# A decoder step's 24-column projection moved from a split weight stream to 16 fp32 matmuls in four column groups

## The chip, the cores and the metric

One core of a Trainium2 chip runs the kernel. The metric is the device time of one execution in microseconds. Three timed runs of the kernel before gave 1956.45, 1956.59 and 1956.63 us; their median is 1956.59.

## The reference

The reference is one layer of a hybrid recurrent decoder for 288 tokens: 256 of a prompt and 8 sequences of 4. The input `x` (288 x 2048) is normalised, scaled and shifted by a condition (the products of `silu(c)` with `w_ada`), and projected by one wide matrix. The projection is then cut into the inputs of three branches:

```
mod = silu(c) @ P['w_ada'] + P['b_ada']
xn = rmsnorm(x, P['g_norm1']) * (1.0 + sc1) + sh1
proj = xn @ P['w_in']
(lru_x, g_q, g_k, g_v, g_lr, g_gate, m_x, m_o, m_if, mg) = jnp.split(proj, _split_points(), axis=-1)
...
logdec = jax.nn.log_sigmoid((g_lr @ P['gla_w_g2'] + P['gla_b_g']).astype(jnp.float32)) / GLA_TAU
...
gates = (m_if + P['ml_b_if']).astype(jnp.float32)
```

All pieces but two are wide (512 to 6144 columns). The two narrow ones are `g_lr`, 16 columns, the low-rank input of the GLA branch's decay, and `m_if`, 8 columns, the input and forget gates of the four mLSTM heads. The change is about these 24 columns. The branches (a linear recurrence "LRU", gated linear attention "GLA" and an mLSTM) are then merged under gates, projected by `w_out`, and followed by a feed-forward block. All of it is in fp32.

## The kernel before

**Layout.** Features lie on the 128 partitions and the 288 tokens along the free axis. `x` is 16 k-tiles of 128 features each.

**Wide projections.** `stream` runs a weight block of 512 columns (four tiles `mm` in PSUM, 128 columns each) over the k-tiles in groups of two. A group's weights are loaded as one 512 KB tile `raw` (L155, `fetch`), split into a high part `hi` by ScalarE (ACT, L164) and a remainder `lo` by VectorE (DVE, L171, `halve`), and each 128 x 128 tile gets three products on TensorE (PE): hi times the high part of the activation (`xh`, L188), hi times its remainder (`xl`, L189) and lo times `xh` (L190). A group of the wide stream thus has 2 k-tiles x 4 column tiles x 3 = 24 products. `raw`, `hi` and `lo` have three buffers each. When a block's last product is done, DVE adds it to what earlier stages left (L576, `added_to`) or another function takes it up.

**Conditions.** The weights of the condition come in units of 1 MB (`fetch_pair`, loads at L381, L368 and L370) that go into spare slots: `ag`, two `st` tiles, or free `s` slots. The letters of a pattern such as `"L L L L . V . L L . V ."` say what `run` does after each group of the stream: L loads the next unit, V visits, that is, runs the products of all units held (fp32 matmuls at L331, four 32-column groups `j` of the array in turn), `.` does nothing. A slot is free for the next unit only when its visit has run.

**Stages.** The normalised `x` becomes final in six stages. In stages 2 to 5 the columns of q, k, v and the LRU's input are computed over the k-tiles of the stage; between the stages DVE and ACT turn the next k-tiles into `xh` and `xl` (L471 to L498). Stage 5 is the last; after it all 16 k-tiles are there. Then comes the narrow projection (`wsm`, one column tile of 128, of which 104 are zeros, 8 k-tiles in a 512 KB load, two loads), and then the "gate stage", the two blocks of `g_gate`, with the pattern `"L L L L . V . ."` and the slots 6, 7, `st` and `ag`. Beside these run the convolution (POOL and DVE, L667 to L686) and the LRU's recurrence as a side generator that moves on one step with each group.

**Who sets the order.** SyncE (SP) issues the loads in program order; a load whose target is still read waits, and all later loads on SP wait behind it. Loads ahead are thus limited by the order of the program. PE, ACT, DVE and POOL are ordered by a scheduler from the program's priorities.

**The narrow projection and its readers.** The lines, before the change, of the pieces that it touches:

- L771 to L772: `sm` and the `stream` over `wsm`; ACT's copy of the result into `sm`
- L868 on, `gla`: POOL clears the 128-partition tile `wg2` and loads its first 32 partitions; the products at L879 take `wg2` (16 rows of it hold the low-rank weight) and `sm`
- L1153 on, `gate_rows`: POOL makes a 0/1 selector `sel` from columns of `ident`; the product at L1158 takes one head's gate out of `sm` and spreads it over 32 partitions each
- the host's packing of `wsm` (2048 x 128, gates at columns 0, 1, 32, 33, 64, 65, 96 and 97, low-rank columns at 2 to 17) and of `wg2`

Of the kernel before, what the change touches and what calls it, by code (L numbers as in the profile page):

```python
# [8 lines left out]
F32 = mybir.dt.float32  # L9
# [5 lines left out]
P = 128  # L15
D = 2048
KT = D // P
# [4 lines left out]
N = NP + NS  # L22
EPS = 1e-6
BIG = 3.4028235e38
SH1, SC1, GT1, SH2, SC2, GT2 = range(6)
# [28 lines left out]
def trunk(ctx, tc, io):  # L54
# [18 lines left out]
    def nm(s):  # L73
        uid[0] += 1
        return f"{s}_{uid[0]}"
# [7 lines left out]
    def misc():  # L83
        return px.tile([P, 512], F32, tag="px", name=nm("px"))
# [157 lines left out]
    def run(gen):  # L242
        for _ in gen:
            if pace["every"]:
                if pace["n"] >= 0:
                    step(pace["every"][pace["n"] % len(pace["every"])])
                pace["n"] += 1
            for g in list(side):
                with tc.high_priority(), ExitStack() as behind:
                    for e in ("last", "lo", "hi"):  # L250
                        behind.enter_context(tc.issue_after(pace[e].ins))
                    if next(g, side) is side:
                        side.remove(g)
# [152 lines left out]
    def visit(n=99):  # L406

        for _ in range(min(n, len(held))):
            name, raw, products, end = held.pop(0)
            products(raw)  # L410
            if end:
                end()
                done.add(name)

    def step(cs):
        for c in cs:
            if c == "L":
                load_one()
            elif c == "F":
                fetched.append(fetch(*ahead_of.pop(0)))  # L420
            elif c.isdigit():
                with tc.high_priority(), tc.issue_after(pace["last"].ins):
                    visit(int(c))
            elif c == "V":
                with tc.high_priority(), tc.issue_after(pace["last"].ins):
                    visit()

    def drain(n):
        while n not in done:
# [126 lines left out]
    qk, vv, lx = slot(8), slot(9), slot(2)  # L556
    early = [(B_Q, qk, 0), (B_Q + 1, qk, 4), (B_Q + 2, vv, 0), (B_Q + 3, vv, 4), (B_LRU, lx, 0), (B_LRU + 1, lx, 4)]
    kept = []

    def start_of(j, onv=(0,)):  # L560

# [61 lines left out]

    a, w = COFF["eye"]
    for i, turn, p in ((2, (5, 4, 0, 1, 2, 3), "F2LL F1FL 2FLL 1 2 ."), (3, (3, 2, 1, 0, 4, 5), "L L . L LV . L L . LLV . ."),
                       (4, (5, 4, 0, 1, 2, 3), "L L . L LV . L L . LLV . ."), (5, (3, 4, 5, 0, 1, 2), "L L L L . V . L L . V .")):
        k0, k1, _ = STAGES[i]
        if i == 5:
            slots.update(ids=(3, 4, None, 5, 6, 7), n=0)
        pace.update(hpins=pace["copies"][-1:])  # L630
        lead = begin(i, p)
        if i < 5:
            with tc.issue_after(pace["lo"].ins):
                for k in range(k1, STAGES[i + 1][1], 2):
                    normalize(k, 2)
        if i == 2:
            ahead_of.extend((win, early[j][0], 1) for j in turn[1:])
            step("FLL")
        else:
            assert not held and not fetched and not ahead_of  # L640
        if i == 4:
            for t, n, r in ((con, "con", slice(0, a)), (con, "con", slice(a + w, CW)), (par, "par", slice(112, PW))):
                G.tensor_copy(t[:, r.start:r.start + 1], mod[:, SC1, 8, 0:1])
                G.dma_start(t[:, r], io[n][:, r])
        take, kept = kept, []
        xh1, mods = pace["xh"], pace["mod"]
        for n, j in enumerate(turn):
            pace["pins"] = pace["adds"][-5:-4] + [mods] * (n > 0)
            if n == 1:
                pace["hpins"] = [xh1]  # L650
            evac = start_of(5, (0, 2)) if i == 2 and n == 0 else added_to(j)
            run(stream(win, early[j][0], act1, k1, evac, k0=k0, take=None if n else take,
                       keep=kept if n == 5 and i < 5 else None, first=() if n else lead))
# [114 lines left out]
    lru_ = beside(lru())  # L768


    sm = cp.tile([P, N], F32, tag="sm", name="sm")  # L771
    run(stream(io["wsm"], 0, act1, KT, lambda m, p: S.copy(sm, p), width=P, kg=8))  # L772
    sg = slot(2)

    def gate_silu(base):
# [92 lines left out]
    def gla():  # L868
        kk_, g_cs, ee = slot(3), slot(4), slot(5)
        wg2 = flat(kk_)[:, 4 * N:4 * N + 512]  # L870
        G.memset(wg2, 0.0)
        G.dma_start(wg2[0:32], io["wg2"])
        rm = resets(row("gc"), 0.0, 1.0, 64)
        bg = Pm("bg")
        yield
# [273 lines left out]
    def gates():  # L1149
        lf, gc, ar, mr, rt = (row(n) for n in ("lf", "gc", "ar", "mr", "rt"))  # L1150
        one, big_ = resets(row("rr"), 0.0, 1.0, NP), None

        def gate_rows(i):  # L1153

            p = misc()
            sel = t288()[:, 0:P]
            G.tensor_copy(sel.rearrange("p (h i) -> p h i", h=4), ident.rearrange("p (h i) -> p h i", h=4)[:, :, i:i + 1].to_broadcast([P, 4, 32]))
            T.matmul(p[:, :N], sel, sm, start=True, stop=True)  # L1158
            return p

        pf = gate_rows(1)
        softlog(lf, pf[:, :N], Pm("bf"), rt)
        pI = gate_rows(0)
        V.tensor_scalar(ar, pI[:, :N], Pm("bi"), None, ALU.add)
        yield
        S.activation(rt, rt, AF.Exp, scale=-1.0)
        S.activation(rt, rt, AF.Ln, bias=1.0)
        yield
        V.tensor_tensor(out=lf, in0=lf, in1=rt, op=ALU.subtract)
        V.tensor_tensor_scan(gc, one, lf, 0.0, ALU.mult, ALU.add)  # L1170
        yield
        V.tensor_tensor(out=ar, in0=ar, in1=gc, op=ALU.subtract)
        big_ = resets(row("lf"), -BIG, 0.0, NP)
        m0 = Pm("m0")
        V.tensor_copy(rt, ar)
        V.tensor_scalar(rt[:, 0:1], ar[:, 0:1], 0.0, None, ALU.max)
        V.tensor_tensor(out=rt[:, NP:N:TS], in0=ar[:, NP:N:TS], in1=m0, op=ALU.max)
        yield
        V.tensor_tensor_scan(mr, big_, rt, 0.0, ALU.add, ALU.max)
        gm = gc  # L1180
        V.tensor_tensor(out=gm, in0=gc, in1=mr, op=ALU.add)
        yield
        mo_ = sc([P, 9], "mout", 1)
        G.tensor_copy(mo_[:, 0:1], gm[:, NP - 1:NP])
        G.tensor_copy(mo_[:, 1:9], gm[:, NP + 3:N:TS])
        G.dma_start(io["o_m"], mo_)
        xr = gm
        S.activation(xr, gm, AF.Exp, scale=-1.0)
        V.tensor_scalar(rt[:, 0:NP], ar[:, 0:NP], mr[:, NP - 1:NP], None, ALU.subtract)

        def bt(a):
            return a.rearrange("p (b t) -> p b t", b=NB)

        mrs = bt(mr[:, NP:N])
        V.tensor_tensor(out=bt(rt[:, NP:N]), in0=bt(ar[:, NP:N]), in1=mrs[:, :, 3:4].to_broadcast([P, NB, TS]), op=ALU.subtract)
        wr = rt
        S.activation(wr, rt, AF.Exp)
        yield
        srow = sc([P, 3, NS], "srow", 1)
        V.tensor_tensor(out=bt(srow[:, 2, :]), in0=m0.unsqueeze(2).to_broadcast([P, NB, TS]), in1=mrs, op=ALU.subtract)  # L1200
        S.activation(srow[:, 2, :], srow[:, 2, :], AF.Exp)
        V.tensor_copy(srow[:, 0, :], ar[:, NP:N])
        V.tensor_copy(srow[:, 1, :], wr[:, NP:N])
        csr = sc([P, NB], "csr", 1)
        V.tensor_copy(csr, srow[:, 2, 3:NS:TS])
        V.tensor_tensor(out=srow[:, 0:2], in0=srow[:, 0:2], in1=eye.unsqueeze(1).to_broadcast([P, 2, NS]), op=ALU.mult)
        scol = sc([P, 2], "scol", 1)
        V.tensor_reduce(out=scol, in_=srow[:, 0:2], axis=AX.X, op=ALU.add)
# [574 lines left out]
```

## Time and profile before

| | |
|---|---|
| median of 3 runs | 1956.59 us (1956.45 to 1956.63) |
| the profiled execution's own time | 1956.76 us |
| its span in the trace | 1955.0 us |
| granted TensorE clock | 0.998 |
| PE busy | 1931.4 us, 99% of the span |
| DVE, ACT, POOL busy | 1039.7, 810.4, 235.5 us |
| loads of the small projection | 198.3 and 201.0 us after the span's start |
| copy into `sm` | 220.0 us |
| first reader of `sm` (L879) | 328.4 us |

Times in the views count from the start of the span. In a timeline row the first number is the start in us, the second the time from the start of the row's first instruction to the end of its last, then engine, line, operation, output <- inputs, shapes, and how many instructions the row holds; brackets give the idle time of the engine ahead of the row and what ended it. An fp32 matmul shows as two instructions. PEld is the weight load of a product, SPq the issuing of a DMA. `128*32` in a PE row says that 32 of the array's columns are used at a time, `128*128` that all are.

### The profile page before, as it was taken

To read this page: it belongs to the slowest core of one execution; us is meant where nothing else is said; L and a number is where in the kernel's file an instruction comes from. 1 tells how busy PE (TensorE), PEld (TensorE's weight loads), DVE (VectorE), ACT (ScalarE), POOL (GpSimd) and SP (SyncE) were. 2 spreads that over 40 slices of the span, in tenths; PEclk is the share of its full clock that TensorE was granted. 3 is DMA by queue.
4 is the path that set the end of the run, shared out by engine and by line. 5 is a ranking of instruction groups with operands and counts; after the bars stand their busy time and mean duration, and the time that the engine had idled before them with its cause. 6 is when DMAs were issued, how large, how long until landed. Compare 5 with 4: busy or idle time off the path is not lost.

```text
span 1955.0 us, 35982 instructions
## 1 busy us (share of the span) xinstructions
PE 1931.4 (99%) x15084; PEld 1832.6 (94%) x15084; DVE 1039.7 (53%) x1601; ACT 810.4 (41%) x1127; POOL 235.5 (12%) x335
## 2 busy tenths in 40 slices
PE   7999999999999999999999999999999999999997
PEld 6899889998999999899999899999999999999997
DVE  6665737535673456654444564445454445444565
ACT  4333474444554353443333453443433334343433
POOL 0001000011042112000013330000000000010101
PEclk9999999999999999999999999999999999999999
DMA  9898566557443369876788554444444544444443
GB/s 391 355 349 318 216 253 234 204 183 258 158 163 119 131 204 311 282 260 251 280 316 322 182 205 162 162 162 164 168 171 154 175 173 162 162 162 162 162 167 119
DMA packets 110161, 417.01 MB, mean 213 GB/s; under 512 B 11648, under 2 KB 11824, under 8 KB 106288
## 3 DMA queue, kind: packets, MB, share of 16 engines
q1 hardware_dynamic: 100944, 382.34, 54.5%
q0 software_dynamic: 8048, 28.99, 4.4%
q10 hardware_dynamic: 1008, 3.39, 0.5%
q8 instruction: 118, 1.93, 0.4%
q14 instruction: 43, 0.35, 0.1%
HBM read 397.86 MB, written 16.81 MB: 212 GB/s over the span
## 4 chain that ended last, share of the span: by engine, by line
PE 97%; DVE 1%; DMA 1%; ACT 0%; issue 0%; SPq 0%; DVEq 0%; ACTq 0%
PE mm L188 29%; PE mm L190 28%; PE mm L189 28%; PE pa L331 5%; DMA s<-wad 1%; PE px L1436 0%; PE pi L1428 0%; PE px L735 0%; PE px L978 0%; PE px L1360 0%; PE px L128 0%; PE px L817 0%; DMA raw<-win 0%; PE px L1046 0%; PE px L1370 0%; PE pi L447 0%
## 5 line engine op out<-in xcount | busy, mean ns | idle before, releaser
L171 DVE TENSOR_TENSOR lo<-raw,hi 128x1024 fp32r<-128x1024 f32 x450 | 550.4, 1225 | 547.2 <-ACT hi L164 517.6
L164 ACT ACTIVATE hi<-raw 128x1024 fp32r<-128x1024 f32 x446 | 472.1, 1060 | 801.7 <-PE mm L189 607.3
L188 PE MATMUL mm<-xh,hi 128*128 128x288 f32 x2544 | 749.4, 299 | 0.3 <-ACT xh L473 0.3
L189 PE MATMUL mm<-xl,hi 128*128 128x288 f32 x2544 | 745.7, 296 | 0.3 <-DVE xl L475 0.3
L190 PE MATMUL mm<-xh,lo 128*128 128x288 f32 x2544 | 730.6, 295 | 0.1
L188 PEld LDWEIGHTS mm<-xh,hi 128*128 128x128 f32 x2544 | 474.7, 188 | 19.1 <-issue 10.9
L188 PE MATMUL mm<-s,hi 128*128 128x288 f32 x1664 | 490.6, 297 | 0.0
L189 PE MATMUL mm<-s,hi 128*128 128x288 f32 x1664 | 488.2, 295 | 0.0
L189 PEld LDWEIGHTS mm<-xl,hi 128*128 128x128 f32 x2544 | 476.9, 188 | 2.4 <-DVE xl L475 0.6
L190 PE MATMUL mm<-s,lo 128*128 128x288 f32 x1664 | 476.6, 295 | 0.4 <-DVE lo L171 0.4
L190 PEld LDWEIGHTS mm<-xh,lo 128*128 128x128 f32 x2544 | 472.0, 188 | 1.8 <-issue 0.8
L188 PEld LDWEIGHTS mm<-s,hi 128*128 128x128 f32 x1664 | 311.8, 188 | 5.2 <-issue 4.6
L189 PEld LDWEIGHTS mm<-s,hi 128*128 128x128 f32 x1664 | 312.5, 188 | 0.3
L190 PEld LDWEIGHTS mm<-s,lo 128*128 128x128 f32 x1664 | 308.3, 188 | 0.8 <-DVE lo L171 0.7
L171 DVE TENSOR_TENSOR lo<-s,hi 128x1024 fp32r<-128x1024 f32 x80 | 98.0, 1225 | 113.8 <-ACT hi L164 113.8
L164 ACT ACTIVATE hi<-s 128x1024 fp32r<-128x1024 f32 x80 | 84.9, 1061 | 140.8 <-PE mm L189 140.1
L1612 POOL TENSOR_TENSOR t<-t 128x288 f32<-128x288 f32 x64 | 60.2, 951 | 639.2 <-ACT t L1611 639.2
L576 DVE TENSOR_TENSOR s<-s,mm 128x288 f32<-128x288 f32 x92 | 39.6, 450 | 48.0 <-PE mm L190 47.4
L1628 DVE TENSOR_TENSOR s<-s,mm 128x288 f32<-128x288 f32 x96 | 40.2, 449 | 33.8 <-PE mm L190 32.6
L1132 POOL TENSOR_TENSOR s<-s,t 128x288 f32<-128x288 f32 x32 | 33.9, 1090 | 191.6 <-DVE t L1131 191.5
L331 PE MATMUL pa<-s,silc 128*32 128x64 f32 (+3 forms) x832 | 52.9, 373 | 0.2 <-DMA s<-wad 0.2
L498 DVE TENSOR_TENSOR s<-t,s 128x288 fp32r<-128x288 f32 x64 | 33.8, 568 | 15.5 <-ACT s L497 15.5
(403 smaller groups left out, 1153.4 us busy)
## 6 DMA issues: line engine op xcount, KB each, us to landing
raw<-win SPq DMA_DIRECT2D x188, 512.0 KB, 4.8
raw<-wf SPq DMA_DIRECT2D x176, 512.0 KB, 4.2
s<-wf SPq DMA_DIRECT2D x80, 512.0 KB, 3.5
s<-wada SPq DMA_DIRECT2D x26, 1024.0 KB, 8.0
s<-wad SPq DMA_DIRECT2D x24, 1024.0 KB, 10.1
ag<-wada SPq DMA_DIRECT2D x22, 1024.0 KB, 5.5
raw<-wout SPq DMA_DIRECT2D x32, 512.0 KB, 5.3
st<-wada SPq DMA_DIRECT2D x20, 512.0 KB, 7.2
```

Source lines behind the costliest of these rows:

```text
L164: pace["hi"] = S.activation(hi, raw, AF.Copy)
L171: pace["lo"] = V.tensor_tensor(out=lo[:, r], in0=raw[:, r], in1=hi[:, r].bitcast(F32), op=ALU.subtract)
L188: T.matmul(pss[m][:, :N], hi[:, kk, ms], xh, start=k == k0 and not take, stop=False)
L189: T.matmul(pss[m][:, :N], hi[:, kk, ms], xl, start=False, stop=False)
L190: pace["last"] = T.matmul(pss[m][:, :N], lo[:, kk, ms], xh, start=False, stop=k == kt - 1 and keep is None)
L331: pace["prod"] = T.matmul(ps[32 * j:32 * j + 32, h * w // 4:(h + 1) * w // 4], silu_c(k), v[:, j], start=k == 0 and h == 0, stop=k == KT - ...
L498: pace["mod"] = V.tensor_tensor(out=dst_l[:, r], in0=src[:, r], in1=dst_h[:, r].bitcast(F32), op=ALU.subtract)
L576: pace["adds"].append(V.tensor_tensor(out=dst[:, base + m, :], in0=dst[:, base + m, :], in1=p, op=ALU.add))
L1132: G.tensor_tensor(out=a, in0=a, in1=t, op=ALU.add)
L1612: G.tensor_tensor(out=r, in0=r, in1=r, op=ALU.mult)
L1628: V.tensor_tensor(out=a, in0=a, in1=p, op=ALU.add)
```

## The change

The stream over `wsm` goes. In its place a function `narrow` runs 16 plain fp32 matmuls, one for each k-tile, of 32 columns by 288 tokens. K-tile `k` goes to the column group `k % 4`, so that PSUM's partitions 0 to 31 hold the sum over the k-tiles 0, 4, 8 and 12, the next 32 that over 1, 5, 9 and 13, and so on. The four partial sums are never added by an instruction of their own: the whole 128-partition tile is copied to `sm`, and the consumers' products add them, because their other operand is repeated four times (`wg2` by the host, the selector by `eye[:, i:8:2]` broadcast).

`narrow` is called by a new letter N in stage 5's pattern, right behind the first visit. Its input is the unsplit activation `xin(k)`. Its weights (16 x 32 columns, 256 KB) are loaded into an `st` tile by SP ahead of stage 5's first group. Line numbers behind the insertion move by 11 to 14 (L576 becomes L588, L772's copy L437).

```diff
+            elif c == "N":
+                with tc.high_priority(), tc.issue_after(pace["prod"].ins):
+                    narrow()
...
+    def narrow():
+
+        ps = misc()
+        for k in range(KT):
+            j = k % 4
+            T.matmul(ps[32 * j:32 * j + 32, :N], ws[:, k], xin(k), start=k < 4, stop=k >= KT - 4, skip_group_check=True)
+        S.copy(sm, ps[:, :N])
...
-                       (4, (5, 4, 0, 1, 2, 3), "L L . L LV . L L . LLV . ."), (5, (3, 4, 5, 0, 1, 2), "L L L L . V . L L . V .")):
+                       (4, (5, 4, 0, 1, 2, 3), "L L . L LV . L L . LLV . ."), (5, (3, 4, 5, 0, 1, 2), "L L L L . VN . L L . V .")):
         if i == 5:
             slots.update(ids=(3, 4, None, 5, 6, 7), n=0)
+            ws = sp.tile([P, 1028], F32, tag="st", name=nm("st"), bufs=2)[:, 0:512].rearrange("p (k c) -> p k c", k=KT)
+            Q.dma_start(ws, io["wsm"])
...
-    sm = cp.tile([P, N], F32, tag="sm", name="sm")
-    run(stream(io["wsm"], 0, act1, KT, lambda m, p: S.copy(sm, p), width=P, kg=8))
...
-        G.memset(wg2, 0.0)
-        G.dma_start(wg2[0:32], io["wg2"])
+        G.dma_start(wg2, io["wg2"])
...
-            G.tensor_copy(sel.rearrange("p (h i) -> p h i", h=4), ident.rearrange("p (h i) -> p h i", h=4)[:, :, i:i + 1].to_broadcast([P, 4, 32]))
+            G.tensor_copy(sel.rearrange("p (h i) -> p h i", h=4), eye[:, i:8:2].unsqueeze(2).to_broadcast([P, 4, 32]))
...
-    wsm = np.concatenate([wi[:, 6160:6161], wi[:, 6164:6165], wi[:, 3072:3088], z[:, :14], wi[:, 6161:6162], wi[:, 6165:6166], z,
-                          wi[:, 6162:6163], wi[:, 6166:6167], z, wi[:, 6163:6164], wi[:, 6167:6168], z], 1)
+    wsm = np.zeros((D, 32), np.float32)
+    wsm[:, 0:8] = wi[:, 6160:6168].reshape(D, 2, 4).transpose(0, 2, 1).reshape(D, 8)
+    wsm[:, 8:24] = wi[:, 3072:3088]
...
-        "wg2": np.pad(I["gla_w_g2"][0], ((2, 14), (0, 0))),
+        "wg2": np.tile(np.pad(I["gla_w_g2"][0], ((8, 8), (0, 0))), (4, 1)),
```

The change moves instructions at three places on which the prediction's steps rest. The first is SP's order at the end of stage 4 and the start of stage 5. `raw_…<-win` is a 512 KB group of a wide projection, `s…<-wada` a condition unit. Before:

```order
L155 DMA raw_1968<-win 128x1024
L155 DMA raw_1998<-win 128x1024
L155 DMA raw_2046<-win 128x1024
L370 DMA s_288_2077<-wada 128x2x1024
L155 DMA raw_2079<-win 128x1024
L370 DMA s_292_2113<-wada 128x2x1024
```

The same place now:

```order
L155 DMA raw_1969<-win 128x1024
L155 DMA raw_1999<-win 128x1024
L643 DMA st_2029<-wsm 128x512
L155 DMA raw_2049<-win 128x1024
L370 DMA s_289_2080<-wada 128x2x1024
L155 DMA raw_2082<-win 128x1024
```

The load of the narrow weights has come in ahead of stage 5's first group (`raw_2046`, now `raw_2049`), and its target is one of the `st` tiles that the visit at the end of stage 4 reads.

The second place is SP's order from the end of stage 5 into the gate stage. Before (`raw_2586` is the gate stage's first group, `s_366` the first condition unit loaded in it):

```order
L155 DMA raw_2454<-win 128x1024
L155 DMA raw_2490<-wsm 128x1024
L155 DMA raw_2546<-wsm 128x1024
L155 DMA raw_2586<-win 128x1024
L370 DMA s_366_2616<-wada 128x2x1024
L155 DMA raw_2626<-win 128x1024
L370 DMA s_370_2656<-wada 128x2x1024
L155 DMA raw_2662<-win 128x1024
```

The same place now (`raw_2514` is the gate stage's first group, `s_358` its first condition unit):

```order
L155 DMA raw_2475<-win 128x1024
L155 DMA raw_2514<-win 128x1024
L370 DMA s_358_2544<-wada 128x2x1024
L155 DMA raw_2572<-win 128x1024
L370 DMA s_365_2602<-wada 128x2x1024
L155 DMA raw_2608<-win 128x1024
```

The two `wsm` groups are gone, so one group stands ahead of the first condition unit behind stage 5's last group, where three stood.

The third place is DVE's order in stage 5, where one block ends and the next begins. The L576 rows add the four column tiles `mm` of the block that ends, and `lo_2193` is the remainder of the next block's first group. Before:

```order
L576 TENSOR_TENSOR s_47_276<-s_47_276,mm_2115 128x288
L576 TENSOR_TENSOR s_47_276<-s_47_276,mm_2116 128x288
L171 TENSOR_TENSOR lo_2193<-raw_2191,hi_2192 128x1024
L576 TENSOR_TENSOR s_47_276<-s_47_276,mm_2117 128x288
L171 TENSOR_TENSOR lo_2223<-raw_2221,hi_2222 128x1024
L576 TENSOR_TENSOR s_47_276<-s_47_276,mm_2118 128x288
```

The same place now, with L588 for the adds and `lo_2196` for that remainder:

```order
L588 TENSOR_TENSOR s_47_276<-s_47_276,mm_2118 128x288
L588 TENSOR_TENSOR s_47_276<-s_47_276,mm_2119 128x288
L588 TENSOR_TENSOR s_47_276<-s_47_276,mm_2120 128x288
L588 TENSOR_TENSOR s_47_276<-s_47_276,mm_2121 128x288
L171 TENSOR_TENSOR lo_2196<-raw_2194,hi_2195 128x1024
L171 TENSOR_TENSOR lo_2226<-raw_2224,hi_2225 128x1024
```

All four adds now stand ahead of the remainder.

More of the change, by code (lines that the diff above doesn't have):

```diff
@@ L558, in trunk @@
     kept = []
+    sm = cp.tile([P, N], F32, tag="sm", name="sm")
     def start_of(j, onv=(0,)):
@@ L1744 @@
         "lst": np.ascontiguousarray(flat(fm(I["state_lru_conv"][0]))), "mst": np.ascontiguousarray(flat(fm(I["state_mlstm_conv"][0]))),
-        "wg2": np.pad(I["gla_w_g2"][0], ((2, 14), (0, 0))),
+        "wg2": np.tile(np.pad(I["gla_w_g2"][0], ((8, 8), (0, 0))), (4, 1)),
         "x": np.ascontiguousarray(fm(x)), "ct": np.ascontiguousarray(fm(c)), "par": np.ascontiguousarray(par), "con": _consts(),
-        "wada": np.ascontiguousarray(I["w_ada"][0].reshape(KT, P, 6, 2, 1024).transpose(2, 3, 0, 1, 4)[GT1:]), "wad1": wad1, "win": pack(win), "wsm": pack(wsm, P),
+        "wada": np.ascontiguousarray(I["w_ada"][0].reshape(KT, P, 6, 2, 1024).transpose(2, 3, 0, 1, 4)[GT1:]), "wad1": wad1, "win": pack(win), "wsm": np.ascontiguousarray(wsm.reshape(KT, P, 32).transpose(1, 0, 2)),
         "lruw": np.ascontiguousarray(np.concatenate([I["lru_w_a"][0], I["lru_w_x"][0]], 0).transpose(1, 0, 2)).reshape(P, 2048),
```

## The prediction

> **What bounds the kernel now.** I read the page first: the engines' busy shares, the chain of waits by engine, and the cost rows of the operations that prepare weights.
>
> ```profile
> PE 1931.4 (99%) x15084; PEld 1832.6 (94%) x15084; DVE 1039.7 (53%) x1601; ACT 810.4 (41%) x1127; POOL 235.5 (12%) x335
> ...
> PE 97%; DVE 1%; DMA 1%; ACT 0%; issue 0%; SPq 0%; DVEq 0%; ACTq 0%
> ...
> L171 DVE TENSOR_TENSOR lo<-raw,hi 128x1024 fp32r<-128x1024 f32 x450 | 550.4, 1225 | 547.2 <-ACT hi L164 517.6
> L164 ACT ACTIVATE hi<-raw 128x1024 fp32r<-128x1024 f32 x446 | 472.1, 1060 | 801.7 <-PE mm L189 607.3
> ...
> L576 DVE TENSOR_TENSOR s<-s,mm 128x288 f32<-128x288 f32 x92 | 39.6, 450 | 48.0 <-PE mm L190 47.4
> ```
>
> TensorE is busy for 99% of the span and is 97% of the chain that ended last. So a product taken off TensorE is worth its full pitch, provided that the weights of the next products are there. Preparing a weight group costs 1.06 us on ACT (hi) and then 1.23 us on DVE (lo); on average both are far from full. The question is thus local: what is TensorE's next work after the 48 removed products, and has it been loaded?
>
> The timeline of TensorE gives the pitch of the projection's products and, at L879, the price of full-width fp32 products.
>
> ```profile
> 331.75 0.29 PE L190 MATMUL mm<-s,lo 128*128 128x288 f32 x1
> ...
> 332.15 0.29 PE L190 MATMUL mm<-s,lo 128*128 128x288 f32 x1
> ...
> 332.55 0.29 PE L190 MATMUL mm<-s,lo 128*128 128x288 f32 x1
> 332.68 1.13 PE L879 MATMUL px<-sm,s 128*128 128x288 f32 x4
> 333.44 0.51 PE L188 MATMUL mm<-xh,hi 128*128 128x288 f32 x1
> 333.78 0.29 PE L189 MATMUL mm<-xl,hi 128*128 128x288 f32 x1
> ```
>
> Three products (a hi·xh, a hi·xl and a lo·xh) start every 0.40 us, 0.133 each; a group of 24 takes 3.20 us.
>
> **Removed.** The old small projection is 16 k-tiles x 3 products = 48 products: 48 x 0.133 = 6.40 us on TensorE. Its evacuation stands just where that says:
>
> ```profile
> L772 ACT COPY sm<-mm x1: 400/400/400, 220.0 to 220.0; 128x288 f32<-128x288 f32 x1
> ```
>
> Its two 512 KB loads, two hi and two lo go as well; they ran beside TensorE and their removal alone gains nothing.
>
> **Added.** The narrow projection is 16 fp32 matmuls of 288 columns into four 32-column groups. Two places run fp32 in such groups: L850 (288 columns) and the condition visits of L331 (512 columns), each 8 matmuls, shown as 16 instructions.
>
> ```profile
> 818.33 0.29 PE L190 MATMUL mm<-xh,lo 128*128 128x288 f32 x1
> 818.55 1.18 PE L850 MATMUL px<-s,ones 128*32 128x288 f32 x16
> 819.66 0.40 PE L188 MATMUL mm<-xh,hi 128*128 128x288 f32 x1
> 819.90 0.29 PE L189 MATMUL mm<-xl,hi 128*128 128x288 f32 x1
> ```
>
> ```profile
> 209.60 0.29 PE L190 MATMUL mm<-xh,lo 128*128 128x288 f32 x1
> 209.83 1.92 PE L331 MATMUL pa<-s,silc 128*32 128x512 f32 x16
> 211.68 0.40 PE L188 MATMUL mm<-xh,hi 128*128 128x288 f32 x1
> 211.92 0.29 PE L189 MATMUL mm<-xl,hi 128*128 128x288 f32 x1
> ```
>
> From the product before to the second one after is 1.57 us at L850 and 2.32 us at L331; without the insertion it would be two pitches, 0.27. So the eight cost 1.30 and 2.05 us. The difference, 0.75 us for 224 more columns, makes 0.96 us of columns at 288 and leaves 0.34 for going into and out of this form. The narrow projection comes right behind a visit of the same form, which has paid the 0.34 already: 16 matmuls = 2 x 0.96 = **1.93 us**. Bounds: 0.34 more if it has to be paid again. If the groups did not overlap, L879 is the price: 332.55 to 333.78 is 1.23, less 0.27, for two matmuls, 0.48 each, so 16 x 0.48 = 7.7 us. I take 1.93, since L850 is the same form and width.
>
> Its copy into sm (0.40 us on ACT) is read only from 328 us on. The 128-partition load of wg2 instead of 32 with a memset, and the other selector of the gate rows, are on POOL and its queue and have hundreds of us. Cost 0; without that cover they would be about a microsecond each.
>
> **Given back in the gate stage.** In both kernels the last stage-5 visit (209.83) frees the slots that the next condition loads need, and SP waits for it. Before, three groups (the two of wsm and the first gate group) were loaded ahead of that wait; now only the first gate group is. SP's queue in the timeline, and the hi splits of the gate groups that follow:
>
> ```profile
> 198.28 3.03 SPq L155 DMA_DIRECT2D raw<-wsm  x2
> ...
> 210.96 0.38 SPq L370 DMA_DIRECT2D s<-wada  x1
> 211.44 0.41 SPq L155 DMA_DIRECT2D raw<-win  x1
> 211.90 0.43 SPq L370 DMA_DIRECT2D s<-wada  x1
> 212.41 0.86 SPq L155 DMA_DIRECT2D raw<-win  x1
> ```
>
> ```profile
> 217.26 1.06 ACT L164 ACTIVATE hi<-raw 128x1024 fp32r<-128x1024 f32 x1 [1.77 <-DMA raw<-win]
> 221.05 1.06 ACT L164 ACTIVATE hi<-raw 128x1024 fp32r<-128x1024 f32 x1 [0.68 <-DVE s L686]
> 224.85 1.06 ACT L164 ACTIVATE hi<-raw 128x1024 fp32r<-128x1024 f32 x1 [2.25 <-DVE s L686]
> 228.62 1.06 ACT L164 ACTIVATE hi<-raw 128x1024 fp32r<-128x1024 f32 x1 [2.21 <-DVE s L686]
> 231.20 1.04 ACT L164 ACTIVATE hi<-raw 128x1024 fp32r<-128x1024 f32 x1
> ```
>
> The four splits are 3.79 us apart. That is the queue's rate: each group now comes with 1 MB of condition weights, 1.57 million bytes, and the window over this stretch shows the DMA engines full at 417 GB/s, which makes 3.77 us.
>
> ```profile
> 213.40:219.80 6.40, 6.40 (x51) 6.40 (x50) 5.80 (x11) 3.60 (x5) 0.00 (x0) 1.00 1.02 417
> ```
>
> TensorE takes only 3.20 us for a group, so through these four it lives off its lead. Count in us from the issue of the first condition load (210.96). The splits of gate groups 2 to 5 start at 6.30, 10.09, 13.89 and 17.66, and nothing in the change makes them earlier, for that queue was empty when they were issued. TensorE is back at 0.72 (0.83 with the slower first product) and has 12 products left of stage 5, then before 48 + 24, now only 24. So it reaches gate group 2 at 0.83 + 84 x 0.133 = 12.03 before (no wait), and at 5.63 now. There hi is ready at 6.30 + 1.06 = 7.36: **1.73 us of waiting**. Then TensorE's order has eight hi products (1.07 us) ahead of the first lo product, while lo takes 1.23: 0.16 more. Group 2 ends at 10.72; hi of group 3 is ready at 11.15 (wait 0.43), of group 4 at 14.95 (0.44), of group 5 at 18.72 (0.41), each with 0.16 for lo. Sum 1.73 + 1.28 + 4 x 0.16 = **3.65 us**. Group 6 (hi at 231.20, 20.24 on this count, done at 21.28) is ready before TensorE asks at 22.08; there the loads carry no condition weights and the lead returns. Of 6.40 us this stage keeps 2.75. Bounds: 1.73 if only the first of these waits comes; 7.9 if no hi product covered the lo (4 x 1.07 more). I take 3.65, since the split times of before carry each of its terms.
>
> The Trainium skill ("DMA: Bandwidth & Descriptors", Anatomy of one DMA) gives a transfer about 2.0 us fixed plus its bytes at 436 GB/s; as an estimate from that page the four groups' 6.29 million bytes would land 16.4 us after the first issue, where the split at 17.66 stands here, and the waits would be some 1.2 us shorter, which makes the sum 1955.3 instead of the one below. The measured splits decide, and the sum goes by them.
>
> **Stage 5.** Two edits of order matter here. First, DVE's order now has the lo of the block's first group behind all four adds of the block before, where it was behind the second. The last add can start only 0.16 us (0.29 less a pitch) after the pitch of the last product; add and lo take 0.45 + 1.23; TensorE has eight hi products (1.07 us) meanwhile: 0.16 + 0.45 + 1.23 − 1.07 = **0.76 us**. Bounds 0 (the adds run earlier than the order makes it look) and 1.84 (nothing covers).
>
> Second, SP issues the narrow weights' load into a tile that the stage-4 visit reads, and all stage-5 loads stand behind it.
>
> ```profile
> 149.75 3.53 SPq L155 DMA_DIRECT2D raw<-win  x2
> ...
> 159.18 1.06 ACT L164 ACTIVATE hi<-raw 128x1024 fp32r<-128x1024 f32 x1 [0.54 <-PE mm L189]
> ...
> 160.09 1.05 PE L331 MATMUL pa<-st,silc 128*32 128x256 f32 x16
> ...
> 162.79 0.40 PE L188 MATMUL mm<-xh,hi 128*128 128x288 f32 x1
> ...
> 163.88 1.09 ACT L472 ACTIVATE xh<-s,mod 128x256 fp32r<-128x256 f32 x2 [3.64 <-DVE mod L356]
> ```
>
> And how long the two old loads, each alone in the queue, took to land (the answer on wsm):
>
> ```profile
> DMA to landing us min/median/max: 3.2/3.2/3.2
> ```
>
> The second of the two raws at 149.75 is stage 5's first group, before. It moves behind the read of st, so to about 161.1, and lands a lone 512 KB load (3.2 us, the wsm loads) and half as much again (0.6) later, at 165.0 to 165.4. Its hi stands ahead of the xh conversions on ACT and ends at 166.4, so xh (163.88 before) starts 2.5 us later. TensorE has 48 products from 162.79 on, to 169.2. xh until 167.9, then an xl (0.45, as an add of the same shape) and half a lo (0.6) make 168.95: covered, by 0.2 us. The groups behind it land 3.77 apart and are wanted 3.20 apart: the fifth lands at 180.5 at the latest, its hi ends at 181.5 and TensorE wants it at 169.2 + 12.8 = 182.0, half a microsecond in hand. Cost 0, and above that one us for each us that these loads come later; it is the thinnest cover in this sum, and the third rival is its failure.
>
> **Elsewhere.** The LRU's steps run beside the groups and move two groups on. The only stall that the timeline shows there is this one:
>
> ```profile
> 316.32 0.30 PE L189 MATMUL mm<-s,hi 128*128 128x288 f32 x1
> 317.06 0.40 PE L190 MATMUL mm<-s,lo 128*128 128x288 f32 x1 [0.43 <-DVE lo L171]
> ```
>
> It is 0.6 us; it may go (−0.6) or grow by one step of its kind (+1). I take 0.
>
> **The sum**, against the profiled execution's own 1956.76 us (span 1955.0): −6.40 + 1.93 + 3.65 + 0.76 = −0.06, so 1956.70. The median of the runs is 0.17 lower: **1956.5 us**. A measurement of this kernel tells about 0.2% from no change, 3.9 us; the forecast is no change.
>
> **Rivals.**
>
> 1. *The gain is kept.* If the waits in the gate stage and the 0.76 do not appear, −6.40 + 1.93 = −4.47 stands: 1952.1, faster by just over 0.2%. For it: TensorE is 97% of the chain. Against: the four splits 3.79 us apart with TensorE at 3.20. Chance 0.11.
>
> 2. *The groups do not overlap* in this accumulation, which goes round the four k-tiles instead of repeating one operand as L331 does. The place is the 16 matmuls behind the first stage-5 visit, the price 7.7 us instead of 1.93: +5.8, so 1962.3, slower. Part of it (from 1.93 + 4 = 6 us on) would already decide for slower. Against: L850's sixteen instructions in 1.18 us. Chance 0.07. The Trainium skill ("TensorEngine Tiling (Array Packing)", Key Properties) has a rule on its side of the bound alone: a change of the tiling mode drains TensorE; if a visit and the narrow products counted as different modes, the 0.34 worked out above would be paid once more (1956.8).
>
> 3. *Stage 5 starves.* If SP's wait ends with the visit (162.79) and not with the read of st (161.1), hi, xh and the first products come 1.7 us later and 0.2 us are covered: +1.5, so 1958.0. Each further us of lateness is paid in full, at the first group or at the fifth: 4 us make 1960.3, and beyond 4.2 it is slower by more than a measurement's 0.2%. For it: SP issues its loads in strict order, one row after another. The Trainium skill ("DMA: Bandwidth & Descriptors", Anatomy of one DMA) speaks against the change here: semaphore waits are held by the issuing sequencer, while the DMA engines only consume what is queued. SP's 198.28 row, one entry of 3.03 us for two loads, agrees. Chance 0.15, 0.05 of it past 0.2%.
>
> **How the numbers follow.** The forecast's own case has 0.67, rival 1 0.11, rival 2 0.07, rival 3 0.15. Low end: the waits 1.2 shorter, the 0.76 and the 0.6 at L171 gone, and a little: 1953.3. High end: rival 3 at +3.5, 1960.0. Outside are rival 1, rival 2 and the tail of rival 3. Faster by over 0.2%: 0.11; slower: 0.07 + 0.05 = 0.12; within: 0.77.
>
> **What would show it.** In the profile after: no L190 run for sm; an L436 group of 32 instructions behind the first stage-5 visit, with 1.9 us to the next product (7.7: rival 2). Four waits of TensorE on hi in the gate stage, 1.7 and then about 0.4 us, with splits 3.8 us apart; if they are missing, rival 1. One wait of 0.8 us on lo at a stage-5 block's start. TensorE unbroken from the stage-4 visit to stage 5; a gap before its first group is rival 3. A gap anywhere after 250 us that before lacks would make the prediction wrong in a way that none of these names.

## The result and the profile after

The changed kernel is slower: 1964.24 us (median of 6 runs, 1961.21 to 1965.93) against 1956.81 for the kernel before on the same chip (6 runs, 1956.45 to 1961.13). The ratio is 1.0034, with a 95% interval from 1.0023 to 1.0044; the forecast was 1956.5 and its range ended at 1960.0. The profiled execution took 1963.23 us, its span was 1961.4 against 1955.0, at the same granted clock of 0.998.

The rows of the page after that answer to those of before, the busy shares and the chain by engine:

```profile
PE 1928.8 (98%) x15068; PEld 1827.2 (93%) x15068; DVE 1037.1 (53%) x1599; ACT 805.7 (41%) x1123; POOL 239.0 (12%) x334
...
PE 94%; DMA 3%; DVE 1%; ACT 1%; issue 0%; SPq 0%; DVEq 0%; ACTq 0%
```

TensorE is busy for 2.6 us less, and yet the span is 6.4 longer: its share of the chain fell from 97% to 94%, while that of DMA rose from 1% to 3% and that of ACT from 0% to 1%. The waits of TensorE between 150 and 330 us, after (what waited, for what: us in total, times, longest):

```profile
PE mm L188 <- ACT hi L164: 3.3, 2, 2.0
PE mm L188 <- DVE s L791: 3.2, 1, 3.2
PE mm L188 <- ACT s L1124: 2.0, 1, 2.0
PE mm L190 <- DVE lo L171: 0.5, 1, 0.5
```

The view leaves out idle times under 0.15 us. Counted from the start of one product to the start of the next, less a pitch of 0.133, a wait comes out about 0.16 longer; the text counts in that way from here on. In the kernel before the same question has a single row, 0.4 us behind lo (0.60 in the text's way). The first row is one wait in the gate stage, which the prediction had, and one in stage 5, where it saw weights come just in time. The last row is a late weight group of stage 5 as well. The two in the middle it did not have at all.

Where the 6.4 us come in is read best from landmarks, the starts of TensorE's groups in both timelines (us from the start of the span):

| landmark | before | after | difference |
|---|---|---|---|
| visit at the end of stage 4 | 159.20 | 159.22 | 0.0 |
| first visit of stage 5 | 188.49 | 190.97 | +2.48 |
| products behind it (after: behind the narrow ones) | 192.06 | 196.49 | +4.43 |
| last visit of stage 5 | 209.83 | 214.23 | +4.40 |
| first visit of the gate stage (48 products fewer) | 238.97 | 241.17 | +2.20 |
| products behind the second visit of the gate stage | 281.92 | 281.89 | −0.03 |
| products behind the next visit | 303.09 | 307.45 | +4.36 |
| first product of the LRU branch's projection | 316.09 | 322.48 | +6.39 |
| end of the span | 1955.0 | 1961.4 | +6.4 |

At 282 us the two kernels are level, where the prediction had −0.06. That they agree so well is luck. Up to 241 us stage 5 and the gate stage lost 2.3 us more than was priced (1.7 and 0.55, see below). Between 241 and 282 the changed kernel wins 2.23 back, from 2.20 to −0.03, and the prediction had no such term. This too is the LRU's shift (e8 below, which shifts nothing else, wins 1.8 there): of its two-instruction fp32 products (L735 before, L749 after) two fewer lie ahead of 282, which is 0.97 (285.05 to 286.29 in the changed kernel, less two pitches), and the two that lie inside a visit lengthen it by 2.05 us now and by 3.31 before.

What the result differs by comes in the 40 us behind: two waits of TensorE, 3.35 and 2.16 us, and the 0.97. At 325 us the difference is 5.7, since the kernel before pays its 0.60 behind lo only there. The last 0.7 us come near 940 us, where TensorE pauses for a late hi and lo; that was not followed up.

TensorE's timeline at the five places, after. First the narrow products:

```profile
194.43 2.12 PE L436 MATMUL px<-s,st 128*32 128x288 f32 x32
196.49 0.40 PE L188 MATMUL mm<-xh,hi 128*128 128x288 f32 x1
```

The visit and the narrow products together last from 190.97 to 196.72 (the second product behind), 5.75 us, where the visit alone lasted from 188.49 to 192.30, 3.81. The narrow ones cost 1.94 us.

Stage 5, the wait on the lo of its third group and that on the hi of its fifth:

```profile
175.81 0.30 PE L189 MATMUL mm<-xl,hi 128*128 128x288 f32 x1
176.58 0.40 PE L190 MATMUL mm<-xh,lo 128*128 128x288 f32 x1 [0.47 <-DVE lo L171]
176.81 0.30 PE L188 MATMUL mm<-xh,hi 128*128 128x288 f32 x1
...
182.65 0.29 PE L190 MATMUL mm<-xh,lo 128*128 128x288 f32 x1
184.20 0.40 PE L188 MATMUL mm<-xh,hi 128*128 128x288 f32 x1 [1.26 <-ACT hi L164]
```

The gate stage, its first wait and the splits behind it on ACT:

```profile
220.85 0.29 PE L190 MATMUL mm<-xh,lo 128*128 128x288 f32 x1
223.14 0.40 PE L188 MATMUL mm<-xh,hi 128*128 128x288 f32 x1 [2.00 <-ACT hi L164]
```

```profile
222.03 1.06 ACT L164 ACTIVATE hi<-raw 128x1024 fp32r<-128x1024 f32 x1 [10.56 <-DMA raw<-win]
225.76 1.06 ACT L164 ACTIVATE hi<-raw 128x1024 fp32r<-128x1024 f32 x1 [2.18 <-DMA raw<-win]
229.53 1.06 ACT L164 ACTIVATE hi<-raw 128x1024 fp32r<-128x1024 f32 x1 [1.73 <-DMA raw<-win]
233.29 1.06 ACT L164 ACTIVATE hi<-raw 128x1024 fp32r<-128x1024 f32 x1 [2.20 <-DVE s L700]
```

The splits are 3.75 us apart, as the prediction had it, and TensorE waits for each of them (2.16, 0.25, 0.28 and 0.26 us).

And the two waits that nobody named, with what ACT does in the first:

```profile
292.39 0.29 PE L190 MATMUL mm<-xh,lo 128*128 128x288 f32 x1
295.87 0.40 PE L188 MATMUL mm<-xh,hi 128*128 128x288 f32 x1 [3.19 <-DVE s L791]
...
320.19 0.29 PE L190 MATMUL mm<-xh,lo 128*128 128x288 f32 x1
322.48 0.40 PE L188 MATMUL mm<-s,hi 128*128 128x288 f32 x1 [2.00 <-ACT s L1124]
```

```profile
288.09 0.40 ACT L790 ACTIVATE t<-mm 128x288 f32<-128x288 f32 x1
288.83 1.06 ACT L164 ACTIVATE hi<-raw 128x1024 fp32r<-128x1024 f32 x1 [0.34 <-DMA raw<-win]
289.91 1.28 ACT L752 ACT_TABLE_LOAD   x1
291.20 2.40 ACT L752 ACTIVATE s<-s 128x576 f32<-128x576 f32 x4
293.62 1.28 ACT L790 ACT_TABLE_LOAD   x1
294.92 0.71 ACT L790 ACTIVATE t<-mm 128x288 f32<-128x288 f32 x2
```

L790 is the evacuation of the gate stage's second block (tanh on ACT, then L791 on DVE); four of them empty the four PSUM tiles `mm`, which the next block needs. Between the second and the third now lies L752, the LRU's square root, with a load of ACT's function table ahead of it and one behind: 4.96 us together. In the kernel before the phase came in two parts, three of its four instructions near 276 us and the last, again between two table loads, here; it ended at 285.83, ahead of the first evacuation at 286.22:

```profile
282.55 1.28 ACT L738 ACT_TABLE_LOAD   x1
283.84 0.69 ACT L738 ACTIVATE s<-s 128x576 f32<-128x576 f32 x1
284.55 1.28 ACT L778 ACT_TABLE_LOAD   x1
286.22 0.41 ACT L778 ACTIVATE t<-mm 128x288 f32<-128x288 f32 x1 [0.38 <-PE mm L190]
```

The second wait is of the same kind: the four splits of the LRU's output (L508, L497 before) lie ahead of the copies at L1124 (L1113 before) that free the tiles. ACT before:

```profile
312.39 2.41 ACT L497 ACTIVATE s<-s 128x576 fp32r<-128x576 f32 x4 [2.61 <-DVE s L754]
314.70 1.05 ACT L164 ACTIVATE hi<-raw 128x1024 fp32r<-128x1024 f32 x1
315.65 0.39 ACT L1113 ACTIVATE s<-mm 128x288 f32<-128x288 f32 x1
```

ACT after:

```profile
318.78 2.41 ACT L508 ACTIVATE s<-s 128x576 fp32r<-128x576 f32 x4 [0.84 <-DVE s L768]
321.09 1.04 ACT L164 ACTIVATE hi<-raw 128x1024 fp32r<-128x1024 f32 x1
322.04 0.99 ACT L1124 ACTIVATE s<-mm 128x288 f32<-128x288 f32 x3
```

Before, the splits were over at 314.80, when TensorE's products ahead of the copies were still running (the last starts at 315.82). Now they end at 321.19, while the last of those products starts at 320.19; one more split of a weight group (L164) follows, and the first copy starts at 322.04.

The LRU runs as a side generator, one step for each group of the main stream. The old projection was two groups, and with them two steps went: every later piece of the LRU meets the main stream two groups further on.

### The profile page after: what moved, and what is told of

The parts are those of the page before. It is cut to its first block, busy times and chain, and to the rows that moved or that the text cites. A ratio compares the mean times of both kernels' runs of the same rounds, so it can differ in the third digit from the quotient of the medians.

```text
span 1961.4 us, 35940 instructions
## 1 busy us (share of the span) xinstructions
PE 1928.8 (98%) x15068; PEld 1827.2 (93%) x15068; DVE 1037.1 (53%) x1599; ACT 805.7 (41%) x1123; POOL 239.0 (12%) x334
## 3 DMA queue, kind: packets, MB, share of 16 engines
q8 instruction: 118, 1.93, 0.4%
## 4 chain that ended last, share of the span: by engine, by line
PE 94%; DMA 3%; DVE 1%; ACT 1%; issue 0%; SPq 0%; DVEq 0%; ACTq 0%
PE mm L188 28%; PE mm L190 27%; PE mm L189 27%; PE pa L331 5%; DMA raw<-win 2%; DMA s<-wad 1%; PE px L1447 0%; PE pi L1439 0%; ACT hi L164 0%; PE px L989 0%; PE px L749 0%; PE px L1371 0%; PE px L128 0%; PE px L829 0%; PE px L1057 0%
## 5 line engine op out<-in xcount | busy, mean ns | idle before, releaser
L164 ACT ACTIVATE hi<-raw 128x1024 fp32r<-128x1024 f32 x444 | 470.1, 1060 | 811.1 <-PE mm L189 581.1
L164 ACT ACTIVATE hi<-s 128x1024 fp32r<-128x1024 f32 x80 | 84.9, 1061 | 142.4 <-PE mm L189 141.7
L588 DVE TENSOR_TENSOR s<-s,mm 128x288 f32<-128x288 f32 x92 | 39.5, 452 | 46.7 <-PE mm L190 45.9
```

What stands on the lines that cost most here:

```text
L164: pace["hi"] = S.activation(hi, raw, AF.Copy)
L588: pace["adds"].append(V.tensor_tensor(out=dst[:, base + m, :], in0=dst[:, base + m, :], in1=p, op=ALU.add))
```

## The experiments

Ten kernels were run, each beside the kernel before on the same chip: e1, e3, e6 and e8 on one chip, the other six on another. Ratios are to the kernel before, with 95% intervals.

| run | median us | before, us | ratio |
|---|---|---|---|
| e1_lru_two_ahead | 1958.34 | 1957.08 | 1.0008 (0.9999 to 1.0017) |
| e8_before_lru_late | 1961.26 | 1957.08 | 1.0023 (1.0013 to 1.0033) |
| e3_lead_two | 1964.20 | 1957.08 | 1.0037 (1.0025 to 1.0050) |
| e6_all | 1958.62 | 1957.08 | 1.0008 (0.9999 to 1.0017) |
| e9_three_repairs | 1952.65 | 1956.78 | 0.9978 (0.9969 to 0.9987) |
| e10_lru_visit_early | 1954.14 | 1956.78 | 0.9984 (0.9976 to 0.9993) |
| e11_lru_wsm_later | 1957.32 | 1956.78 | 1.0003 (0.9994 to 1.0012) |
| e7_serial | 1964.54 | 1956.78 | 1.0040 (1.0028 to 1.0053) |
| e12_lru_one_ahead | 1958.23 | 1957.01 | 1.0006 (0.9997 to 1.0015) |
| e14_root_one_later | 1964.43 | 1957.01 | 1.0037 (1.0023 to 1.0051) |

### The LRU's place, undone in the changed kernel: e1_lru_two_ahead

```diff
     lru_ = beside(lru())
+    for _ in range(2):
+        with tc.high_priority(), ExitStack() as behind:
+            for e in ("last", "lo", "hi"):
+                behind.enter_context(tc.issue_after(pace[e].ins))
+            next(lru_)
```

> The changed kernel with the LRU's side generator moved on by two steps ahead of the gate stage, as it was in the kernel before, where the two groups of the removed projection did it. Theory (order on ACT): the two waits of TensorE at 292.4 us (3.35, for an evacuation of the gate stage behind the square-root phase with its two table loads) and at 320.2 us (2.16, for a copy behind four splits) go, the old 0.60 at lo may come back: about 4.9 us less than the changed kernel, 1959 us (1957.5 to 1960.5). Rival (late loads): the raw weights in that stretch land late because of SP's changed order, the LRU has nothing to do with it: 1963 to 1965 us as before.

Measured 1958.34, 5.9 us below the changed kernel's median; between the two profiled executions it is 4.9. Both waits are gone from the trace, and the old 0.60 on lo is back; the gate stage's (2.17 at its first group) and stage 5's (1.44, ended at 183.5 us) are still there. The rival falls.

### The LRU's place alone, in the kernel before: e8_before_lru_late

```diff
-    lru_ = beside(lru())
-
-
     sm = cp.tile([P, N], F32, tag="sm", name="sm")
     run(stream(io["wsm"], 0, act1, KT, lambda m, p: S.copy(sm, p), width=P, kg=8))
+    lru_ = beside(lru())
```

> The kernel before, with nothing changed but that the LRU's side generator joins two groups later, behind the old small projection. Theory (order on ACT): the square-root phase falls between the gate stage's evacuations here too, and TensorE waits 3 to 5 us more: 1960 to 1962 us, slower. Rival (late loads): no load moves here, so no difference: 1956.6 us.

Measured 1961.26, 4.2 us above before, with the same two waits (2.89 and 2.15). The profiled execution's span is 3.5 longer than that of before. Here is the first wait, in this kernel's timeline (L738 and L776 are its square root and evacuation):

```profile
286.37 0.40 ACT L776 ACTIVATE t<-mm 128x288 f32<-128x288 f32 x1
...
287.74 1.28 ACT L738 ACT_TABLE_LOAD   x1
289.03 2.40 ACT L738 ACTIVATE s<-s 128x576 f32<-128x576 f32 x4
291.46 1.28 ACT L776 ACT_TABLE_LOAD   x1
292.75 0.71 ACT L776 ACTIVATE t<-mm 128x288 f32<-128x288 f32 x2
```

```profile
290.68 0.29 PE L190 MATMUL mm<-xh,lo 128*128 128x288 f32 x1
293.70 0.40 PE L188 MATMUL mm<-xh,hi 128*128 128x288 f32 x1 [2.73 <-DVE s L777]
```

Nothing of the narrow projection is in this kernel. The shift by two groups is enough for both waits.

### Which piece of the LRU: e12_lru_one_ahead and e14_root_one_later

The first is e1 without its loop, with one `next(lru_)`; the second leaves the LRU where the change put it and holds back only its end:

```diff
+        yield
         for h in range(4):
             S.activation(tt[:, 2 * h:2 * h + 2], tt[:, 2 * h:2 * h + 2], AF.Sqrt, scale=-0.25)
```

> The changed kernel with the LRU only one step ahead. ACT's order then has the square-root phase ahead of all four evacuations of the gate stage's second block, but the four splits of the LRU's output still ahead of the L1124 copies. Theory (two separate waits, each from what stands ahead of an evacuation on ACT): the wait of 3.35 us near 292 us goes and the one of 2.16 us near 320 us stays: about 3.3 us less than the changed kernel, 1960.5 to 1961.5 us. Rival (one cause, the LRU's chain being late as a whole): both shrink by half, or both stay.

Measured 1958.23. The wait near 292 is gone, the one at the copies is still there with 1.86 us. That is the pattern of two separate waits. In this run the LRU's four splits are over at 315.72 already, and it is two weight splits (L164, to 317.61) that follow them on ACT and hold the copies back: the cause is ACT's order, not the length of the LRU's splits alone. The time is 2.3 us below the expected range, and no higher than e1's although e1 has no such wait. About half of that is stage 5, where this profiled execution lost 0.68 on its waits instead of 2.05. So the reading rests on the trace and not on the time.

> The changed kernel with the LRU's steps from the square root on one group later. ACT's order then has the square-root phase behind all four evacuations and the four splits behind the L1124 copies. Theory: the wait near 292 us goes here too, although the phase is later and not earlier; behind 318 us TensorE waits for the later splits themselves instead of for the copies, about 3 us: 1961 to 1962.5 us. Rival (the LRU's lateness is what costs): slower than the changed kernel, 1965 us or more.

Measured 1964.43, 2 us above the expected range and close to the rival's 1965; the time alone would not decide. In the trace the wait near 292 is gone here too, with the phase later instead of earlier, so it is not lateness that costs there but a place between the evacuations. At the end of the LRU, however, TensorE loses more than I had worked out: 3.45 and 1.62 us for the splits themselves, and another 1.00 at 449 us.

### The lead of the gate stage, by shifting its loads: e3_lead_two and e6_all

```diff
-    every("L L L L . V . .")
+    every("L L L L . V . .", skip=2)
```

> The changed kernel with the gate stage's pattern of condition loads started two groups later, so that three weight groups stand ahead of the first condition load again. Theory (loss of the lead): the four waits on hi between 220 and 236 us, about 4 us in sum, go: their stretch is 4 us shorter; with the LRU's order as in the changed kernel its two waits stay or move, so 1959 to 1962 us in all. Rival (TensorE is slowed there by something else than the lead): the four waits stay.

Measured 1964.20, nothing gained and above the expected range. The four waits between 220 and 236 are gone, as expected, but TensorE waits 4.23 us for a hi near 290. e6_all adds e1's loop and issues the narrow weights' load later (below):

> The changed kernel with three repairs at once: the LRU two steps ahead, the condition loads of the gate stage two groups later, and the narrow weights' load issued behind four groups of stage 5 instead of ahead of the first. Theory: each of the three terms (about 4.9, 4.2 and 2.4 us) comes off, and 1963.2 becomes 1952 to 1953 us, which is the 6.40 less 1.94 that the change was worth on TensorE alone; faster than before by 0.2%. Rival (the terms share their cover, so that one repair only uncovers the next wait): 1955 to 1959 us.

Measured 1958.62: the rival holds. Of TensorE's waits between 150 and 330 us two rows are left in this run:

```profile
PE mm L188 <- ACT hi L164: 4.0, 1, 4.0
PE mm L190 <- DVE lo L171: 0.4, 1, 0.4
```

and the big one stands at 286 us, where ACT waits for a load:

```profile
289.60 1.06 ACT L164 ACTIVATE hi<-raw 128x1024 fp32r<-128x1024 f32 x1 [7.52 <-DMA raw<-win]
```

The shifted pattern moved the gate stage's last visit two groups later as well, and so took from the next stage the lead that it gave to this one: ahead of that visit SP issues three weight groups in a row (254.80 to 263.43) before it has to wait, where e1 has five (253.66 to 270.02).

### The lead from the other side: e10_lru_visit_early, e11_lru_wsm_later and e9_three_repairs

e10 has e1's loop and runs stage 5's last visit two groups earlier; its loads were issued long before. e11 has e1's loop and issues the narrow weights' load behind four groups of stage 5, when its `st` tile is free. e9 has all three (the first pair of lines below is the pattern of stage 5, cut out of a longer line; e1's loop is left out):

```diff
-"L L L L . VN . L L . V ."
+"L L L L W VN L L V . . ."
...
-            Q.dma_start(ws, io["wsm"])
...
+            elif c == "W":
+                Q.dma_start(ws, io["wsm"])
```

> As the kernel with the LRU two steps ahead, and the last visit of stage 5 two groups earlier; the narrow weights' load stays ahead of stage 5's first group. Theory: the gate stage's waits go (about 4.2 us off 1958.3: 1954.2 us), those of stage 5 (about 2.4 us) stay. Rival (shared cover): 1957 to 1959 us.

Measured 1954.14. The gate stage's waits are gone, and none has come up behind.

> As the kernel with the LRU two steps ahead, and the narrow weights' load behind four groups of stage 5. Theory (the load's wait on its buffer holds stage 5's loads back): TensorE's wait of 1.4 us on a late fifth group near 182 us and the smaller ones beside it go, about 2.4 us off 1958.3: 1955.9 us. Rival (the fifth group is late by itself, a slow transfer): the wait stays, 1958.3 us.

Measured 1957.32, 1.0 us below e1 (which ran on the other chip) instead of 2.4; stage 5 runs there without a wait, but see below on how much there was to gain. DVE's order where the fifth group starts a block is back to that of before as well: the lo of the fifth group stands between the adds again (181.87, ahead of the add at 183.00). So both terms of stage 5 hang on the place of this one load. The gate stage still waits (2.22 us at its first group).

> The LRU two steps ahead and the narrow weights' load behind four groups of stage 5, as in the run with all repairs before; but the lead of the gate stage comes from the other side: the last visit of stage 5 runs two groups earlier, so that three weight groups again stand between it and the first condition load, and the gate stage's own pattern is as it was. Theory (a lead given at one end is taken at the other when the pattern is shifted, and is not when only the visit is): no wait on hi at 220 us and none at 286 us; 1957.1 - 6.4 + 1.9 = 1952.6 us (1952 to 1954), faster than before by 0.2%. Rival (the gate stage's loads take 3.8 us a group whatever stands ahead, and someone pays for it): 1956 to 1959 us.

Measured 1952.65, as worked out, 4.1 us below before: ratio 0.9978 (0.9969 to 0.9987). The chain's row of its page and all that TensorE waits for between 150 and 330 us:

```profile
PE 97%; DVE 2%; ACT 0%; DMA 0%; issue 0%; DVEq 0%; SPq 0%; ACTq 0%
```

```profile
PE mm L190 <- DVE lo L171: 0.4, 1, 0.4
```

It is the one row that the kernel before has too. This version beats both kernels.

### The column groups: e7_serial

On top of e1's loop, which is left out here:

```diff
-            j = k % 4
-            T.matmul(ps[32 * j:32 * j + 32, :N], ws[:, k], xin(k), start=k < 4, stop=k >= KT - 4, skip_group_check=True)
-        S.copy(sm, ps[:, :N])
+            j = 0
+            T.matmul(ps[32 * j:32 * j + 32, :N], ws[:, k], xin(k), start=k == 0, stop=k == KT - 1, skip_group_check=True)
+        V.memset(sm, 0.0)
+        S.copy(sm[0:32], ps[0:32, :N])
```

> As the kernel with the LRU two steps ahead, but the 16 narrow products all go to the first column group, one after another (sm's other three quarters are cleared). If column groups overlap, as the trace of the changed kernel has it (1.9 us for the 16), this costs 16 x 0.48 = 7.7 us instead of 1.9: 5.8 us more than 1958.3, 1964.1 us. If what is saved came from the narrow weights alone and not from the overlap: 1958.3 us.

Measured 1964.54, 6.2 us above e1. The row of the narrow products says it directly:

```profile
193.25 7.92 PE L436 MATMUL px<-s,st 128*32 128x288 f32 x32
```

7.92 us against 2.12 in four groups: the groups do run at the same time, and the saving is theirs.

## Why the prediction was wrong, step by step

**The step that failed is "Elsewhere. The LRU's steps run beside the groups and move two groups on ... I take 0".** Its bounds, −0.6 and +1, came from the one stall that the trace of before shows there, as if a shift of the LRU could only change that one. It moved a 4.96 us phase of ACT from ahead of four evacuations to between them, and four splits from a time at which TensorE had work left to one at which it needed the copies behind them. The pieces stand in the trace of before: the table loads (1.28 us each), the four square roots and the splits. What was not asked is what they would stand ahead of after the shift.

Measured on the waits alone: 3.35 + 2.16 − 0.60 = +4.9 us in the changed kernel's trace, and 2.89 + 2.15 − 0.60 = +4.4 in e8's. Part of it comes back where the LRU's products lie more cheaply between TensorE's other work, so that the shift alone, e8, costs +3.5 in the spans of the profiled executions and +4.2 in the median. Taking it back, in e1, gives −4.9 in the spans and −5.9 in the median. With the term out, as e1 has it, the change measures 1958.34, which is inside the forecast's range and within 0.1% of before.

**Removed, 6.40, and added, 1.93.** Right: the narrow products cost 1.94, and e9 without the waits is 4.1 below before, where 6.40 − 1.93 = 4.47 was the most that could come. The prediction took from the Trainium skill ("TensorEngine Tiling (Array Packing)", Key Properties) that a change of the tiling mode drains TensorE. The trace agrees with how it weighed that: the narrow products behind a visit paid no second 0.34, so the two count as one mode.

**Given back in the gate stage, 3.65.** The mechanism was right: lead lost, splits 3.75 apart. The size was 4.20 (the landmarks: 6.40 − (4.40 − 2.20)). The first wait was 2.16 instead of 1.73, as the first split came 6.67 us after the first condition load's issue (215.36) instead of 6.30, and each of the eight restarts costs 0.10 more (below). The 436 GB/s of the Trainium skill ("DMA: Bandwidth & Descriptors", Anatomy of one DMA) would have made it shorter, not longer. That section gives its figures for loads issued by GpSimd, and these go out on SP's queue; the trace has 418 GB/s over this stretch, and no run that has these waits shows them 1.2 us shorter, as the forecast's low end had them:

```profile
218.80:233.20 14.40, 12.20 (x83) 10.99 (x82) 8.68 (x15) 5.15 (x7) 0.00 (x0) 1.00 1.02 418
```

**Stage 5, 0.76.** The wait on the lo of the fifth group, behind all four adds, was sized rightly: in e7, e10, e12 and e14 it is 0.76, 0.77, 0.68 and 0.69, here in e10:

```profile
183.77 0.40 PE L190 MATMUL mm<-xh,lo 128*128 128x288 f32 x1 [0.61 <-DVE lo L171]
```

The changed kernel's profiled execution does not show it, since there the hi of that group comes later still. The stretch lost 2.48, because the loads came late: the second group's hi starts 4.74 us behind the first's (4.11 in e10), so that the third group's lo is 0.63 late (176.58), and the fifth group's hi follows the fourth's by 5.11 us, by 3.73 in e10. The second is the point at which the prediction saw half a microsecond in hand:

```profile
177.98 1.06 ACT L164 ACTIVATE hi<-raw 128x1024 fp32r<-128x1024 f32 x1 [2.71 <-DMA raw<-win]
183.09 1.06 ACT L164 ACTIVATE hi<-raw 128x1024 fp32r<-128x1024 f32 x1 [4.06 <-DMA raw<-win]
```

```profile
176.97 1.06 ACT L164 ACTIVATE hi<-raw 128x1024 fp32r<-128x1024 f32 x1 [2.69 <-DMA raw<-win]
180.70 1.06 ACT L164 ACTIVATE hi<-raw 128x1024 fp32r<-128x1024 f32 x1 [2.67 <-DMA raw<-win]
```

With the load moved, in e11 and e9, stage 5 has no wait at all. That the load's wait on its buffer takes the cover away is thus shown; what made the fifth transfer slow in some runs is not.

**Rivals.** The first (gain kept) was out by the gate stage's waits. The second (no overlap) is excluded by e7. The third (stage 5 starves) did not meet its condition: the narrow load went out at 160.79, with the read of st, and the first products came in time (162.82). Its effect came all the same, at the third and the fifth group, with 1.7 us more than the 0.76. What the prediction's last sentence named as outside all of them, a gap behind 250 us that before lacks, is what came.

## What to carry to other kernels

Work that is paced by another stream's steps moves when steps of that stream go, even if nothing of it was touched: before taking steps out, look in the changed order at what the paced work now stands ahead of on each engine, evacuations of PSUM above all. Loads that an earlier stream covered need their lead back; give it by making buffers free earlier, since a pattern shifted as a whole only hands the wait to the next stage. A saving on the engine that bounds the kernel is worth its full pitch only when what follows is already there, and here three small repairs made that of a loss: 1964.2 to 1952.7 us.

## What the runs showed of the hardware

After each wait TensorE's first product is followed only 0.24 us later by the next instead of 0.13 (184.20 to 184.44, 223.14 to 223.37): about 0.10 us more for every restart. In the gate stage, with four waits on hi and four on lo, that makes 0.8 us.

The changed kernel's times spread over 4.7 us (1961.21 to 1965.93) and e9's over 1.5 (1951.91 to 1953.38). Of the profiles with the narrow load ahead of stage 5, three have the slow fifth transfer (the changed kernel, e1 and e3, 4.95 to 5.17 us behind the fourth) and four have not (e7, e10, e12 and e14, 3.7). Those four ran on another chip than e1 and e3, so whether it goes by the execution or by the chip is open, and so is how much of the spread it makes.
